# Stick-breaking attention with a fixed TensorE order, paired heads and three units of lookahead

## The chip, the cores and the metric

The program runs on one core of a Trainium2 chip. The metric is the device time of one execution in microseconds, the median of several runs. Its engines, each with an instruction queue of its own, are TensorE (PE; its weight loads are the rows PEld), VectorE (DVE), ScalarE (ACT), GpSimd (POOL) and SyncE (SP), which issues the transfers.

## The reference, cut to what matters

A transformer of two layers, width 1024, sequence 2048. The first layer mixes three kinds of attention; the change touches one of them, stick-breaking, in 6 of its 16 heads. For a block of 128 queries, z are the scaled scores; the weight of a key is sigmoid(z) times the product of sigmoid(-z) over all later keys that are still before the query:

```python
strict = key_idx[None, :] < q_idx[:, None]
log_1mb = jnp.where(strict, jax.nn.log_sigmoid(-z), 0.0)
rc = jnp.flip(jnp.cumsum(jnp.flip(log_1mb, axis=-1), axis=-1), axis=-1)
after = rc - log_1mb
w = jnp.where(strict, jnp.exp(jax.nn.log_sigmoid(z) + after), 0.0)
return jnp.einsum('bhqk,bkhd->bqhd', w.astype(v.dtype), v)
```

## The kernel before, in words

Two layers are written as a row of stages. The stick-breaking stage, `stick_breaking`, follows the projections of layer 0 and is followed by `differential`. It loops over 3 pairs of heads (p), 4 chunks of 512 queries (t, from 3 down to 0), 4 blocks of 128 queries in a chunk (qi) and the chunks of up to 512 keys (c) at or below the diagonal, the last one first. One pass of the innermost loop, for both heads of the pair, is called a **unit** here: 120 of them, 84 of 512 keys, and 12 each of 384, 256 and 128 keys. A **block** is 128 queries by 128 keys of one head; the stage has 816.

For each head a unit does the following (names as in the rows below):

- the scores `psz` = queries (`qs`) times keys (`kv`), two matmuls into one PSUM bank, and on the 48 diagonal units a third that adds the mask (L572, L575);
- on ScalarE, `wb` = sigmoid(z) into SBUF (L577) and sigmoid(-z) in place in PSUM (L578);
- on VectorE, a scan from the last key to the first that keeps the running product in `row` (L581); its second operand is a broadcast zero in SBUF;
- `wb` times `row` (L585), four times on GpSimd and once on VectorE in turn (`"PPPPV"`);
- the transposes of the 128x128 blocks into one PSUM bank `pstp` on TensorE (`tblocks`, L474) and their copy into `wT`, on ScalarE (L121) and VectorE (L123) in turn (`"AV"`);
- `pspv` += values times `wT` (L591), two matmul records per block.

At the end of a chunk VectorE multiplies `pspv` by the loaded gate `sl` (L595) and the result is stored. PSUM's eight banks are z 4, tp 3, pv 1; SBUF has 5 buffers each of `row`, `wb` and `wT`.

A scheduler orders each engine's instructions, TensorE's among them, from the program and its own estimate of times. So rows of other work can stand between those of this stage: `filler` prepares `differential`, and its casts of output weights (`wo`, L871 on ScalarE) are drawn up to the start of the stage. A `PinnedCore` wrapper, already in use in `differential`, keeps the named engines in the order of the program; instructions sent through it carry the helper's line (L57 in the changed kernel).

Of the kernel before, what the change touches and what calls it, by code (L numbers as in the profile page):

```python
# [7 lines left out]
F32 = mybir.dt.float32  # L8
# [3 lines left out]
AF = mybir.ActivationFunctionType  # L12
ALU = mybir.AluOpType
# [4 lines left out]
P = 128  # L18
NB = S // P
TC = 512  # L20
NT = S // TC
# [11 lines left out]
FT = 1  # L33
# [3 lines left out]
GROUPS = ((), (), (0, 1), (2, 3), (4,), (), (), (), (5, 6))  # L37
EVAC_C = "A"
FILL = 0.95
PRODUCTS = ((), (0, 1), (), (2, 3))  # L40
SHUF_D = [4, 5, 6, 7, 0, 1, 2, 3] + list(range(8, 32))
SHUF_S = [8, 9, 10, 11, 12, 13, 14, 15, 0, 1, 2, 3, 4, 5, 6, 7] + list(range(16, 32))
# [22 lines left out]
class Net:  # L65
# [47 lines left out]
    def turn(self, key, pattern):  # L113

        k = self.turns.get(key, 0)
        self.turns[key] = k + 1
        return pattern[k % len(pattern)]
# [164 lines left out]
    def layer1_proj(self):  # L282
        nc, dr = self.nc, self.dr
# [3 lines left out]
        ws = [w0, w1]  # L287
# [29 lines left out]
        for k, dst in enumerate((0, 1, self.sbq[1], self.sbk[1], self.sbq[2], self.sbk[2])):  # L317
            w = nxt
            for t in range(NT):
                ps = self.proj_t(w, t)  # L320
                if k < 2:
                    q = self.t("c2")
                    nc.scalar.mul(q, ps, 0.125)
                    for hh in range(2):
                        qs = self.t("c2", F32R)
# [14 lines left out]
        ws = [nxt, None]  # L340
# [10 lines left out]
        for p in range(3):  # L351
            for base, dst in ((9, self.dfq), (12, self.dfk)):
                w = nxt
                for t in range(NT):
# [3 lines left out]
                    hi = self.t("c2", F32R)  # L358
                    lo = self.t("c2", F32R)
# [5 lines left out]
                           [(f, t) for f in range(6) for t in range(NT)] + [(f, t) for t in range(NT) for f in (6, 7)])  # L365
        for k, _ in enumerate(gates):
            if k == 24 + GATES_A:
                self.sb_first = self.load_sb(0)

    def rope_all(self):  # L370

# [154 lines left out]

    def load_sb(self, p):

        qs = self.load_qstack(self.sbq[p], NT - 1)
        ks = [self.t("kv", F32R) for _ in range(2)]  # L530
        n = S if p else TC
        for lo in range(S - n, -1, -n):
            for hh in range(2):
                for part in range(2):
                    self.dma(ks[hh][64 * part:64 * part + 64, lo:lo + n], self.sbk[p][part, 64 * hh:64 * hh + 64, lo:lo + n])
        vp = self.t("kv", F32, [P, NB, P])
        self.dma(vp, self.v1[:, :, p * P:(p + 1) * P].rearrange("b k f -> k b f"))
        return ks, vp, qs

    def stick_breaking(self):  # L540
        nc = self.nc
        for p in range(3):
            ks, vp, qs = self.load_sb(p) if p else self.sb_first
            for t in range(NT - 1, -1, -1):
                if p == 2 and t == FT:
                    self.fill = self.filler()
                    for f in next(self.fill):
                        f()
                    self.dk, self.dq = {}, {}
                    self.load_dq(0, 0, 0)  # L550
                    for c in range(NT - 1):
                        self.load_dk(0, c)
                if t < NT - 1:
                    qs = self.load_qstack(self.sbq[p], t)
                sl = self.load_silu(self.silu[p], t)
                pv = self.psum("pv")
                for qi in range(3, -1, -1):
                    qb = 4 * t + qi
                    qcol = slice(qi * P, (qi + 1) * P)
                    n = (qb + 1) * P  # L560
                    pr = [self.t("row") for _ in range(2)]
                    for hh in range(2):
                        nc.gpsimd.memset(pr[hh][:, n - 1:n], 1.0)
                    for c in range(qb // 4, -1, -1):
                        lo, hi = c * 512, min(n, c * 512 + 512)
                        m = hi - lo
                        ws = []
                        for hh in range(2):
                            z = self.psum("z")
                            diag = hi == n  # L570
                            for k in range(2):
                                nc.tensor.matmul(z[:, :m], qs[:, hh, k, qcol], ks[hh][:, lo:hi], start=(k == 0),  # L572
                                                 stop=(k == 1 and not diag))
                            if diag:
                                nc.tensor.matmul(z[:, m - P:m], self.identb, self.mask[:, 2 * P + 1:3 * P + 1], start=False, stop=True)  # L575
                            w = self.t("wb")
                            nc.scalar.activation(w[:, :m], z[:, :m], AF.Sigmoid, scale=0.125)  # L577
                            nc.scalar.activation(z[:, :m], z[:, :m], AF.Sigmoid, scale=-0.125)  # L578
                            s0 = 1 if lo == 0 else 0
                            prr = pr[hh]  # L580
                            nc.vector.tensor_tensor_scan(  # L581
                                prr[:, lo + s0 - 1:hi - 1][:, ::-1], z[:, s0:m][:, ::-1], self.zero.to_broadcast([P, m - s0]),
                                prr[:, hi - 1:hi], ALU.mult, ALU.add)
                            eng = nc.gpsimd if self.turn("mul", "PPPPV") == "P" else nc.vector
                            eng.tensor_mul(w[:, :m], w[:, :m], prr[:, lo:hi])  # L585
                            ws.append(w)
                        wT = [self.tblocks([w[:, j * P:(j + 1) * P] for j in range(m // P)]) for w in ws]
                        for j in range(m // P):
                            blk = c * 4 + j
                            for hh in range(2):  # L590
                                nc.tensor.matmul(pv[64 * hh:64 * hh + 64, qcol], vp[:, blk, 64 * hh:64 * hh + 64],  # L591
                                                 wT[hh][:, j * P:(j + 1) * P],
                                                 start=(hi == n and j == 0), stop=(c == 0 and j == m // P - 1))
                mt = self.t("c2")
                nc.vector.tensor_mul(mt, pv, sl)  # L595
                self.dma(self.m1[p, :, t * TC:(t + 1) * TC], mt, nc.scalar if p == 2 and t == 0 else None)

    def differential(self):

# [763 lines left out]
    def run(self):  # L1363
        nc, dr, i = self.nc, self.dr, self.i
        with self.phase({"kv": 6, "qs": 2}, {}):
            with self.phase({"big": 8, "w": 13, "c2": 9, "mv": 2}, {"mm": 3, "z": 2, "tp": 2, "pv": 1}):
                self.layer1_proj()
            right = ExitStack()
            right.enter_context(self.phase({"rx": 3, "mp": 5, "wo": 5, "kc": 3, "qa": 2}, {}, "right"))
            with self.phase({"row": 5, "wb": 5, "wT": 5, "c2": 2, "sl": 2}, {"z": 4, "tp": 3, "pv": 1}, "right"):  # L1370
                self.stick_breaking()
        self.rp = dr.tile([NB, P, D], F32, name="rp")
        self.silu2 = [dr.tile([P, S], F32, name=f"silu2_{f}") for f in range(8)]
        self.m2 = dr.tile([8, P, S], F32, name="m2")
        with self.phase({"c2": 3, "sl": 2}, {}):
            with self.phase({"qd": 2, "wT": 7, "vc": 4, "row": 9, "kd": 3},
                            {"mm": 1, "z": 3, "tp": 2, "pv": 2}):
                tail = self.differential()
            right.close()
            with self.phase({"big": 16}, {}):  # L1380
                with self.phase({"w": 4, "raw": 1}, {"mm": 5, "tp": 3}):
                    with self.phase({"ex": 1, "m": 2, "mp": 4, "rx": 5, "gb": 2}, {}):
                        self.join(tail)
                    with self.phase({"w": 6, "cs": 2, "c2": 7}, {}):
                        self.layer2_kv()
                        for _ in self.gates(i["wo"][11:19], self.silu2, order=[(f, t) for f in range(2, 7) for t in range(NT)] + [(7, 3), (7, 0)]):
# [80 lines left out]
```

## Time and profile before

| | us |
|---|---|
| median of 3 runs (lowest to highest) | 2593.26 (2591.59 to 2594.64) |
| profiled execution: its time | 2590.89 |
| profiled execution: its span | 2589.1 |
| stick-breaking stage, from 720 to 1117 of the span | 397 |

The profiled execution stands for 0.09% less than the median. The stage is one part of the whole program, so shares over the whole span say little about it; the rows below are cut to its window. Busy times of TensorE come from pipelined matmuls whose ends are modelled, so that a PE near 100% busy is not a PE at its peak. "Idle before" of a group is the time for which its engine had nothing to do just ahead of it, with what ended that wait.

### The profile page before, as it was taken

The numbers are of one execution on the slowest core, as the hardware profiler recorded it, in microseconds if no ns is written. First come the engines' busy times: TensorE is split into PE (matmuls) and PEld (weight loads), VectorE is DVE, ScalarE is ACT, GpSimd is POOL, SyncE is SP. The second block draws the span as 40 slices with busy tenths as digits, with TensorE's granted clock in tenths as the row PEclk, the third lists the DMA queues.
The fourth block names the chain that finished last, engine by engine and source line by source line (L and its number), as shares of the span: only waits on it lengthen the run. The fifth ranks groups of instructions, "written<-read, shape, count | busy, mean of one in ns | idle before, by whom it ended". The sixth has DMA issues, their size and how long they took to land. (4 is left out here: it accounts for less than half of the span.)

```text
span 2589.1 us, 42439 instructions
## 1 busy us (share of the span) xinstructions
PE 2450.0 (95%) x15564; PEld 1952.1 (75%) x15564; DVE 1626.6 (63%) x3744; ACT 1261.8 (49%) x2653; POOL 897.5 (35%) x752
## 2 busy tenths in 40 slices
PE   8999999999979999989888889899999999999998
PEld 7778998888857777757666667778788777777887
DVE  4833223531159999979899899795311776677455
ACT  4442222221147777747777677543211777776200
POOL 0401003750036655620110121364621655534333
PEclk9999999999989999989999999999999999999999
DMA  7643222331571422263454332463323555523541
GB/s 287 208 158 129 74 84 90 126 126 48 140 177 42 107 50 50 58 161 99 107 123 123 99 98 63 147 207 128 82 90 116 146 161 155 149 93 106 194 146 65
DMA packets 199247, 311.59 MB, mean 120 GB/s; under 512 B 17920, under 2 KB 97280, under 8 KB 198528
## 3 DMA queue, kind: packets, MB, share of 16 engines
q1 hardware_dynamic: 198464, 307.83, 40.2%
q8 instruction: 123, 2.02, 0.3%
q10 hardware_dynamic: 576, 1.05, 0.1%
q14 instruction: 84, 0.69, 0.1%
HBM read 204.74 MB, written 104.07 MB: 119 GB/s over the span
## 5 line engine op out<-in xcount | busy, mean ns | idle before, releaser
L55 PE MATMUL psmm<-big,w 128*128 128x512 f32 x1680 | 413.8, 394 | 0.0
L55 PEld LDWEIGHTS psmm<-big,w 128*128 128x128 f32 x1680 | 305.8, 189 | 57.6
L581 DVE TENSOR_TENSOR_SCAN row<-psz,row,zero 128x512 f32<-128x512 f32 (+5 forms) x240 | 258.6, 1108 | 34.1 <-ACT psz L578 33.8
L252 PE MATMUL psmm<-big,w 128*128 128x512 f32 x1200 | 275.2, 389 | 0.0
L585 POOL TENSOR_TENSOR wb<-wb,row 128x512 f32<-128x512 f32 (+3 forms) x192 | 219.3, 1152 | 133.0 <-DVE row L581 123.1
L252 PEld LDWEIGHTS psmm<-big,w 128*128 128x128 f32 x1200 | 225.0, 188 | 47.0 <-issue 0.2
L55 PE MATMUL psmm<-big,mp 128*128 128x512 f32 x1056 | 245.0, 392 | 1.4 <-POOL big L962 1.4
L55 ACT ACTIVATE row<-row,mn 128x2048 f32<-128x2048 f32 (+7 forms) x192 | 229.8, 1202 | 11.8 <-DVE mn L728 7.3
L55 PEld LDWEIGHTS psmm<-big,mp 128*128 128x128 f32 x1056 | 198.4, 189 | 43.0 <-POOL big L962 1.8
L722 DVE TENSOR_SCALAR_CACHE_REDUCE row<-psz 128x512 f32<-128x512 f32 (+1 forms) x324 | 200.5, 639 | 25.1 <-PE psz L55 24.5
L1181 DVE TENSOR_TENSOR c<-psmm,c 128x512 f32<-128x512 f32 x62 | 42.7, 691 | 240.3 <-ACT c L1180 240.2
L55 ACT COPY wT<-pstp 128x512 f32<-128x512 f32 (+3 forms) x240 | 121.0, 522 | 116.7 <-PE pstp L55 114.0
L591 PE MATMUL pspv<-wT,kv 128*64 128x128 f32 x1632 | 158.0, 287 | 17.2 <-ACT wT L121 17.2
L892 POOL TENSOR_TENSOR mp<-mp,mp 128x640 fp32r<-128x640 f32 x32 | 52.2, 1632 | 347.4 <-ACT mp L55 297.3
L577 ACT ACTIVATE wb<-psz 128x512 f32<-128x512 f32 (+3 forms) x240 | 129.8, 541 | 53.5 <-PE pstp L474 38.4
L591 PEld LDWEIGHTS pspv<-wT,kv 128*64 128x64 f32 x1632 | 106.7, 139 | 62.3 <-issue 20.7
L572 PE MATMUL psz<-kv,qs 128*128 128x512 f32 (+3 forms) x480 | 150.0, 406 | 2.1 <-DVE row L581 2.0
L55 PE MATMUL psmm<-wo,mp 128*128 128x512 f32 x480 | 148.0, 421 | 3.2 <-ACT mp L55 2.5
L764 DVE SCALAR_TENSOR_TENSOR row<-row,tiny,row 128x128 f32<-128x128 f32 (+7 forms) x144 | 149.9, 1090 | 0.4
L1180 ACT ACTIVATE c<-psmm 128x512 f32<-128x512 f32 x62 | 36.7, 596 | 211.7 <-PE psmm L252 203.8
L207 POOL TENSOR_TENSOR w<-w,w 128x1024 fp32r<-128x1024 f32 x20 | 48.6, 2432 | 257.5 <-ACT w L206 154.5
L55 PE MATMUL pstp<-ident,row 128*128 128x128 f32 x816 | 130.1, 280 | 6.6 <-ACT wT L55 5.6
(220 smaller groups left out, 5073.6 us busy)
## 6 DMA issues: line engine op xcount, KB each, us to landing
silu<-c SPq DMA_DIRECT2D x54, 256.0 KB, 2.3
sl<-silu SPq DMA_DIRECT2D x54, 256.0 KB, 3.2
qs<-sbq SPq DMA_DIRECT2D x48, 256.0 KB, 5.3
cs<-rope SPq DMA_DIRECT2D x24, 512.0 KB, 4.4
kc<-k SPq DMA_DIRECT2D x36, 320.0 KB, 5.0
w<-in_we_dram SPq DMA_DIRECT2D x20, 512.0 KB, 3.7
raw<-in_wo_dram SPq DMA_DIRECT2D x20, 512.0 KB, 3.9
rx<-in_x_dram SPq DMA_DIRECT2D x32, 256.0 KB, 2.8
```

What stands on the lines that cost most here:

```text
L55: return self.tc.keep_in_program_order(f(*a, **k))
L207: eng.tensor_sub(lo[:, sl], raw[:, sl], hi[:, sl].bitcast(F32))
L252: self.nc.tensor.matmul(ps, w[a][:, c, :], self.xpart(t, c, b), start=(c == k == 0), stop=(c == 7 and k == 2))
L572: nc.tensor.matmul(z[:, :m], qs[:, hh, k, qcol], ks[hh][:, lo:hi], start=(k == 0), stop=(k == 1 and not diag))
L577: nc.scalar.activation(w[:, :m], z[:, :m], AF.Sigmoid, scale=0.125)
L581: nc.vector.tensor_tensor_scan(prr[:, lo + s0 - 1:hi - 1][:, ::-1], z[:, s0:m][:, ::-1], self.zero.to_broadcast([P, m - s0]), prr[:, hi - ...
L585: eng.tensor_mul(w[:, :m], w[:, :m], prr[:, lo:hi])
L591: nc.tensor.matmul(pv[64 * hh:64 * hh + 64, qcol], vp[:, blk, 64 * hh:64 * hh + 64], wT[hh][:, j * P:(j + 1) * P], start=(hi == n and j == ...
L722: nc.vector.tensor_scalar(e[:, col + lo:col + lo + n0], z[:, :n0], -scale, before, ALU.mult, ALU.min, accum_out=acc)
L764: self.nc.vector.scalar_tensor_tensor(x[:, lo:hi], y[:, lo:hi], cf[hh][:, w:w + 1], x[:, lo:hi], ALU.mult, ALU.add)
L892: self.nc.gpsimd.tensor_sub(ml, m, mh.bitcast(F32))
L1181: nc.vector.tensor_mul(sg, ps, sg)
```

## The change

The stage is written as three functions over a flat list of units: `scores` (matmuls, sigmoids, scan, product), `turn` (transposes and their copies) and `values`. `scores` runs three units ahead of `turn`; `values` follows for two units at a time. TensorE is pinned to this order. The two heads' scores stand in one tile of two banks, so that one ACTIVATE of up to 128x1024 does both heads; the second sigmoid goes into an SBUF tile `s` and not back into PSUM; the zeros of the scan are a PSUM tile; all products are on GpSimd; two copies of three are on ScalarE (`"AAV"`). The queries of the next chunk are loaded at the start of a chunk, and the keys and values of the next pair at the start of t = 2.

```python
-                            w = self.t("wb")
-                            nc.scalar.activation(w[:, :m], z[:, :m], AF.Sigmoid, scale=0.125)
-                            nc.scalar.activation(z[:, :m], z[:, :m], AF.Sigmoid, scale=-0.125)
...
-                                prr[:, lo + s0 - 1:hi - 1][:, ::-1], z[:, s0:m][:, ::-1], self.zero.to_broadcast([P, m - s0]),
...
-                            eng = nc.gpsimd if self.turn("mul", "PPPPV") == "P" else nc.vector
-                            eng.tensor_mul(w[:, :m], w[:, :m], prr[:, lo:hi])
...
+        self.nc = PinnedCore(nc, self.tc, ("tensor",))
...
+        def begin(p, t):
+            sls[p, t] = self.load_silu(self.silu[p], t)
+            k = chunks.index((p, t)) + 1
+            if k < len(chunks):
+                qs[chunks[k]] = self.load_qstack(self.sbq[chunks[k][0]], chunks[k][1])
+            if t == NT - 2 and p < 2:
+                kv[p + 1] = self.load_sb(p + 1)
...
+            z = self.psum("z", [P, 2, 512])
+            for hh in range(2):
+                for k in range(2):
+                    self.nc.tensor.matmul(z[:, hh, :m], qs[p, t][:, hh, k, qi * P:(qi + 1) * P], kv[p][0][hh][:, lo:hi], start=(k == 0),
+                                          stop=(k == 1 and not diag))
...
+            w = ws[u] = self.t("wb", F32, [P, 2, 512])
+            nc.scalar.activation(w[:, :, :m], z[:, :, :m], AF.Sigmoid, scale=0.125)
+            rest = self.t("s", F32, [P, 2, 512])
+            nc.scalar.activation(rest[:, :, :m], z[:, :, :m], AF.Sigmoid, scale=-0.125)
+            for hh in range(2):
+                prr = prs[p, t, qi][hh]
+                nc.vector.tensor_tensor_scan(
+                    prr[:, lo + s0 - 1:hi - 1][:, ::-1], rest[:, hh, s0:m][:, ::-1], zero.to_broadcast([P, m - s0]),
+                    prr[:, hi - 1:hi], ALU.mult, ALU.add)
+                nc.gpsimd.tensor_mul(w[:, hh, :m], w[:, hh, :m], prr[:, lo:hi])
...
+            wTs[u] = [self.tblocks([w[:, hh, j:j + P] for j in range(0, hi - lo, P)], "AAV") for hh in range(2)]
...
+        for u in units[:SB_AHEAD]:
+            scores(u)
+        for k, u in enumerate(units):
+            if k + SB_AHEAD < len(units):
+                scores(units[k + SB_AHEAD])
+            turn(u)
+            while k - done >= SB_GROUP or k == len(units) - 1 and done <= k:
+                for v in units[done:done + SB_GROUP]:
+                    values(v)
+                done += SB_GROUP
...
-            with self.phase({"row": 5, "wb": 5, "wT": 5, "c2": 2, "sl": 2}, {"z": 4, "tp": 3, "pv": 1}, "right"):
+            with self.phase({"row": 4, "wb": 4, "s": 3, "wT": 7, "c2": 2, "sl": 2}, {"z": 2, "tp": 2, "pv": 1, "zero": 1}, "right"):
```

TensorE's queue before, in the first chunk of the first pair (waits on semaphores in brackets, named by the engine that signals):

```order
L572 MATMUL psz_6580<-kv_5725,qs_6520 128x512 [waits DVE_49]
L572 MATMUL psz_6580<-kv_5725,qs_6520 128x512
L474 MATMUL pstp_6495<-ident,wb_6482 128x128 [waits PE_49,Pool_49]
L474 MATMUL pstp_6495<-ident,wb_6482 128x128 x3
L591 MATMUL pspv_5908<-wT_6462,kv_5742 64x128 [waits Activation_49]
L572 MATMUL psz_6610<-kv_5724,qs_6520 128x512 [waits DVE_49]
L572 MATMUL psz_6610<-kv_5724,qs_6520 128x512
L591 MATMUL pspv_5908<-wT_6469,kv_5742 64x128 [waits DVE_49]
L591 MATMUL pspv_5908<-wT_6462,kv_5742 64x128
```

Scores of one head, transposes and values of another unit follow one another in an order that the scheduler chose; a score tile waits for the scan (VectorE) that read its bank. In the changed kernel the queue at that place reads:

```order
L57 MATMUL pstp_6080<-ident,wb_5968 128x128 [waits Activation_49,Pool_49]
L57 MATMUL pstp_6080<-ident,wb_5968 128x128 x3
L57 MATMUL pstp_6087<-ident,wb_5968 128x128 [waits DVE_49,Pool_49]
L57 MATMUL pstp_6087<-ident,wb_5968 128x128 x3
L57 MATMUL psz_6094<-kv_5724,qs_5719 128x512 x2
L57 MATMUL psz_6094<-kv_5725,qs_5719 128x512 x2
L57 MATMUL pstp_6107<-ident,wb_6001 128x128 [waits Activation_49,Pool_49]
L57 MATMUL pstp_6107<-ident,wb_6001 128x128 x2
L57 MATMUL pstp_6113<-ident,wb_6001 128x128 [waits Activation_49,Pool_49]
L57 MATMUL pstp_6113<-ident,wb_6001 128x128 x2
L57 MATMUL pspv_6050<-wT_6041,kv_5742 64x128
L57 MATMUL pspv_6050<-wT_6048,kv_5742 64x128
```

Here both heads' transposes stand together, each waiting for the copy that freed its `pstp` tile (two tiles in all) and for the product; the scores of a later unit stand between the transposes of two units, and the values of two units behind the second.

ScalarE's queue before, at that place:

```order
L577 ACTIVATE wb_6156<-psz_6153 128x512 [waits Pool_49]
L578 ACTIVATE psz_6153<-psz_6153 128x512 [waits DVE_49]
L577 ACTIVATE wb_6186<-psz_6183 128x512 [waits DVE_49,PE_49]
L578 ACTIVATE psz_6183<-psz_6183 128x512 [waits DVE_49]
L121 COPY wT_6128<-pstp_6123 128x512 [waits PE_49]
L577 ACTIVATE wb_6194<-psz_6191 128x512 [waits Pool_49]
L578 ACTIVATE psz_6191<-psz_6191 128x512 [waits DVE_49]
```

And in the changed kernel (L591 and L593 are its two sigmoids, L123 its copy, L909 the cast of an output weight):

```order
L123 COPY wT_6041<-pstp_6036 128x512 [waits PE_49]
L909 CAST wo_9784<-rx_9776 128x512 [waits DMAHW3_49]
L591 ACTIVATE wb_6072<-psz_6067 128x1024 [waits PE_49,Pool_49]
L593 ACTIVATE s_6074<-psz_6067 128x1024 [waits DVE_49,Activation_49]
L123 COPY wT_6085<-pstp_6080 128x512 [waits PE_49]
L123 COPY wT_6092<-pstp_6087 128x512 [waits PE_49,Activation_49]
L591 ACTIVATE wb_6099<-psz_6094 128x1024 [waits PE_49,Pool_49]
```

One pair of wide sigmoids takes the place of two pairs; a unit's copies stand behind the sigmoids of the unit three further on, and ahead of those of the fourth. The casts stay at the start of the stage.

## Rows read from the trace of the kernel before

**Rows 1.** Windows: us; busy (x) of PE, PEld, DVE, ACT, POOL; PEclk; DMA share; GB/s

```profile
720.00:760.00 40.00, 21.05 (x123) 14.59 (x122) 18.09 (x20) 16.50 (x33) 15.33 (x19) 0.79 1.00 228
760.00:1117.00 357.00, 356.65 (x2907) 257.86 (x2905) 334.59 (x402) 261.25 (x574) 217.36 (x275) 0.99 0.25 59
720.00:1117.00 397.00, 377.71 (x3028) 272.45 (x3026) 352.69 (x421) 277.75 (x607) 232.68 (x293) 0.97 0.32 76
```

**Rows 2.** Lines, 720 to 1117: count | busy us, mean ns | idle before, what ended it

```profile
L581 DVE TENSOR_TENSOR_SCAN row<-psz,row,zero 128x512 f32<-128x512 f32 (+5 forms) x240 | 258.6, 1108 | 34.1 <-ACT psz L578 33.8
L585 POOL TENSOR_TENSOR wb<-wb,row 128x512 f32<-128x512 f32 (+3 forms) x192 | 219.3, 1152 | 133.0 <-DVE row L581 123.1 <-PE pspv L591 4.4 <-PE pstp L474 4.0
...
L123 DVE COPY wT<-pstp 128x512 f32<-128x512 f32 (+3 forms) x120 | 70.5, 591 | 7.5 <-PE pstp L474 7.0
...
L585 DVE TENSOR_TENSOR wb<-wb,row 128x512 f32<-128x512 f32 (+3 forms) x48 | 34.3, 714 | 1.0
```

**Rows 3.** Waits, 760 to 1117: who waited for what, us in total, times, longest

```profile
POOL wb L585 <- DVE row L581: 119.9, 116, 3.7
ACT wT L121 <- PE pstp L474: 39.9, 62, 2.1
...
DVE row L581 <- ACT psz L578: 22.1, 25, 6.8
PEld pstp L474 <- issue: 20.8, 120, 0.3
```

**Rows 4.** Lines by form, ScalarE alone, 720 to 1117

```profile
L578 ACT ACTIVATE psz<-psz 128x512 f32<-128x512 f32 x168 | 101.7, 606 | 0.0
L577 ACT ACTIVATE wb<-psz 128x512 f32<-128x512 f32 x168 | 101.7, 605 | 45.9 <-PE pstp L474 36.7 <-PE psz L572 7.3 <-PE psz L575 0.9
L121 ACT COPY wT<-pstp 128x512 f32<-128x512 f32 x84 | 49.6, 591 | 33.0 <-PE pstp L474 32.0
...
L577 ACT ACTIVATE wb<-psz 128x128 f32<-128x128 f32 x24 | 6.7, 281 | 5.8 <-POOL wb L585 2.6 <-PE psz L575 1.5 <-PE pstp L474 1.3
```

**Rows 5.** Timeline of ScalarE, first 40 us: start, duration, instruction, [idle before]

```profile
739.43 1.66 ACT L871 CAST wo<-rx 128x512 fp32r<-128x512 f32 x3 [12.96 <-DMA m<-c]
...
757.67 0.62 ACT L871 CAST wo<-rx 128x512 fp32r<-128x512 f32 x1 [6.68 <-DMA rx<-in_woute_dram]
```

**Rows 6.** Timeline of all engines, 849 to 863

```profile
849.83 0.71 PE L572 MATMUL psz<-kv,qs 128*128 128x512 f32 x2
...
850.63 0.60 ACT L577 ACTIVATE wb<-psz 128x512 f32<-128x512 f32 x1 [0.78 <-PE psz L572]
...
851.13 0.59 ACT L578 ACTIVATE psz<-psz 128x512 f32<-128x512 f32 x1
...
851.49 0.66 PE L474 MATMUL pstp<-ident,wb 128*128 128x128 f32 x4
...
852.43 1.21 PE L572 MATMUL psz<-kv,qs 128*128 128x512 f32 x4
...
853.65 0.65 PE L591 MATMUL pspv<-wT,kv 128*64 128x128 f32 x6
...
855.88 0.33 PE L474 MATMUL pstp<-ident,wb 128*128 128x128 f32 x1
...
857.03 1.09 PE L591 MATMUL pspv<-wT,kv 128*64 128x128 f32 x14
```

**Rows 7.** Instructions of L585: duration ns min/median/max, first and last start, forms

```profile
L585 POOL TENSOR_TENSOR wb<-wb,row x192: 454/1273/1367, 724.2 to 1114.0; 128x512 f32<-128x512 f32 x144, 128x256 f32<-128x256 f32 x18, 128x384 f32<-128x384 f32 x15, 128x128 f32<-128x128 f32 x15
...
L585 DVE TENSOR_TENSOR wb<-wb,row x48: 280/692/1153, 729.3 to 1114.8; 128x512 f32<-128x512 f32 x24, 128x384 f32<-128x384 f32 x9, 128x128 f32<-128x128 f32 x9, 128x256 f32<-128x256 f32 x6
```

**Rows 8.** Lines by form, 760 to 1117: full-width scan, product, transposes

```profile
L585 POOL TENSOR_TENSOR wb<-wb,row 128x512 f32<-128x512 f32 x137 | 173.6, 1276 | 110.8 <-DVE row L581 102.9 <-PE pspv L591 4.4 <-PE pstp L474 3.0
...
L474 PE MATMUL pstp<-ident,wb 128*128 128x128 f32 x783 | 129.2, 284 | 0.0
...
L581 DVE TENSOR_TENSOR_SCAN row<-psz,row,zero 128x512 f32<-128x512 f32 x83 | 104.2, 1272 | 16.0 <-ACT psz L578 15.9
```

More of the change, by code (lines that the diff above doesn't have):

```diff
@@ L39 @@
 FILL = 0.95
+SB_AHEAD = 3
+SB_GROUP = 2
 PRODUCTS = ((), (0, 1), (), (2, 3))
@@ L367, in layer1_proj @@
             if k == 24 + GATES_A:
-                self.sb_first = self.load_sb(0)
+                qs = self.load_qstack(self.sbq[0], NT - 1)
+                self.sb_first = (*self.load_sb(0), qs)
     def rope_all(self):
@@ L527, in load_sb @@
     def load_sb(self, p):
-        qs = self.load_qstack(self.sbq[p], NT - 1)
         ks = [self.t("kv", F32R) for _ in range(2)]
@@ L537, in load_sb @@
         self.dma(vp, self.v1[:, :, p * P:(p + 1) * P].rearrange("b k f -> k b f"))
-        return ks, vp, qs
+        return ks, vp
     def stick_breaking(self):
         nc = self.nc
[L542 to L575, printed above, removed]
-                            w = self.t("wb")
-                            nc.scalar.activation(w[:, :m], z[:, :m], AF.Sigmoid, scale=0.125)
-                            nc.scalar.activation(z[:, :m], z[:, :m], AF.Sigmoid, scale=-0.125)
-                            s0 = 1 if lo == 0 else 0
-                            prr = pr[hh]
-                            nc.vector.tensor_tensor_scan(
-                                prr[:, lo + s0 - 1:hi - 1][:, ::-1], z[:, s0:m][:, ::-1], self.zero.to_broadcast([P, m - s0]),
-                                prr[:, hi - 1:hi], ALU.mult, ALU.add)
-                            eng = nc.gpsimd if self.turn("mul", "PPPPV") == "P" else nc.vector
-                            eng.tensor_mul(w[:, :m], w[:, :m], prr[:, lo:hi])
[L586 to L593, printed above, removed]
@@ new lines, in stick_breaking @@
+        self.nc = PinnedCore(nc, self.tc, ("tensor",))
+        chunks = [(p, t) for p in range(3) for t in range(NT - 1, -1, -1)]
+        units = [(p, t, qi, c) for p, t in chunks for qi in range(3, -1, -1) for c in range(t, -1, -1)]
+        kv, qs, sls, prs, ws, wTs, pvs = {0: self.sb_first[:2]}, {(0, NT - 1): self.sb_first[2]}, {}, {}, {}, {}, {}
+        def begin(p, t):
[5 more added lines that the diff above has]
+                kv[p + 1] = self.load_sb(p + 1)
+            if p == 2 and t == FT:
+                self.fill = self.filler()
+                for f in next(self.fill):
+                    f()
+                self.dk, self.dq = {}, {}
+                self.load_dq(0, 0, 0)
+                for c in range(NT - 1):
+                    self.load_dk(0, c)
@@ new lines, in bounds, with scores @@
+        def bounds(u):
+            p, t, qi, c = u
+            n = (4 * t + qi + 1) * P
+            return n, c * 512, min(n, c * 512 + 512)
+        def scores(u):
+            p, t, qi, c = u
+            n, lo, hi = bounds(u)
+            m, diag, s0 = hi - lo, hi == n, int(lo == 0)
+            if qi == 3 and c == t:
+                begin(p, t)
+            if c == t:
+                prs[p, t, qi] = [self.t("row", F32, [P, 2048]) for _ in range(2)]
+                for hh in range(2):
+                    nc.gpsimd.memset(prs[p, t, qi][hh][:, n - 1:n], 1.0)
+            z = self.psum("z", [P, 2, 512])
[3 more added lines that the diff above has]
+                                          stop=(k == 1 and not diag))
+                if diag:
+                    self.nc.tensor.matmul(z[:, hh, m - P:m], self.identb, self.mask[:, 2 * P + 1:3 * P + 1], start=False, stop=True)
+            w = ws[u] = self.t("wb", F32, [P, 2, 512])
+            nc.scalar.activation(w[:, :, :m], z[:, :, :m], AF.Sigmoid, scale=0.125)
+            rest = self.t("s", F32, [P, 2, 512])
+            nc.scalar.activation(rest[:, :, :m], z[:, :, :m], AF.Sigmoid, scale=-0.125)
+            for hh in range(2):
+                prr = prs[p, t, qi][hh]
[3 more added lines that the diff above has]
+                nc.gpsimd.tensor_mul(w[:, hh, :m], w[:, hh, :m], prr[:, lo:hi])
@@ new lines, in turn, with values @@
+        def turn(u):
+            n, lo, hi = bounds(u)
+            w = ws.pop(u)
+            wTs[u] = [self.tblocks([w[:, hh, j:j + P] for j in range(0, hi - lo, P)], "AAV") for hh in range(2)]
+        def values(u):
+            p, t, qi, c = u
+            n, lo, hi = bounds(u)
+            if qi == 3 and c == t:
+                pvs[p, t] = self.psum("pv")
+            pv, wT, nj = pvs[p, t], wTs.pop(u), (hi - lo) // P
+            for j in range(nj):
+                for hh in range(2):
+                    self.nc.tensor.matmul(pv[64 * hh:64 * hh + 64, qi * P:(qi + 1) * P], kv[p][1][:, 4 * c + j, 64 * hh:64 * hh + 64],
+                                          wT[hh][:, j * P:(j + 1) * P], start=(hi == n and j == 0), stop=(c == 0 and j == nj - 1))
+            if qi == 0 and c == 0:
@@ L594, in stick_breaking @@
                 mt = self.t("c2")
-                nc.vector.tensor_mul(mt, pv, sl)
+                nc.vector.tensor_mul(mt, pvs.pop((p, t)), sls.pop((p, t)))
                 self.dma(self.m1[p, :, t * TC:(t + 1) * TC], mt, nc.scalar if p == 2 and t == 0 else None)
+        done = 0
+        zero = self.psum("zero")[:, :1]
+        nc.vector.memset(zero, 0.0)
+        for u in units[:SB_AHEAD]:
[8 more added lines that the diff above has]
+                done += SB_GROUP
@@ L598, in differential @@
+        self.nc = nc
     def differential(self):
```

## The prediction

> **What bounds the kernel now.** I read the windows first, since shares over the whole program mix stages. The stage takes 397 us, of which VectorE is busy 352.69; in the stretch from 760 to 1117 it is busy 334.59 of 357, or 94% [rows 1]. TensorE reads as busy all the time there, but its matmuls are pipelined, so that says little. GpSimd is busy 217 us, ScalarE 261.
>
> The lines and the waits tell the same engine from the other side. GpSimd's 133 us of idle time before its products end almost all with a scan of VectorE [rows 2]; in the stretch it waits for `row` 116 times, 119.9 us in all [rows 3]. ScalarE waits for transposes (39.9 us ahead of its copies), which wait for products. VectorE itself waits 22.1 us for a sigmoid [rows 3]. So VectorE sets the pace: 258.6 us of scans, 70.5 of copies, 34.3 of products [rows 2]. The reader should see one engine that hardly waits and others that wait for it.
>
> The first 40 us are another matter: VectorE is busy 18 us of them [rows 1], and ScalarE stands twice behind a cast of output weights whose data has not landed, for 12.96 and 6.68 us [rows 5]. These casts stand at the stage's start in the changed order too, behind the same loads, so I give this stretch no gain and no loss, within 3 us.
>
> **The change part by part.** *VectorE* loses its 48 products (34.3 us) and 40 of its 120 copies (one in three instead of one in two: 70.5/3 = 23.5 us) [rows 2]. That is 57.8 us, of which 97% lie in the stretch: 334.6 - 56 = 279 us. It would no longer be full.
>
> *GpSimd* gets those 48 products. Its own cost 1152 ns in the mean [rows 2], so 48 x 1.15 = 55 us, and 217 + 54 = 271 us in the stretch. That lies beside the rest as long as the stretch stays longer than that.
>
> *ScalarE.* No 1024-wide sigmoid is in the trace. From 128 to 512 columns one goes from 281 to 605 ns [rows 4], 0.844 ns a column, so 1024 columns give 605 + 512 x 0.844 = 1037 ns. Consecutive ones start 0.50 apart [rows 6], 0.1 less than one lasts, so about 0.93 for the pair of heads. The price has two sides: two of today's take 2 x 0.50 = 1.00, and a fixed share (281 - 128 x 0.844 = 173 ns) saved whole and not overlapped at all would make it 1.00 - 0.17 = 0.83. I take 0.93, as the line through two widths is nearest. ScalarE also gets 40 more copies at 0.53 to 0.59 us [rows 4]; with 1.87 for the sigmoids and 4/3 x 0.5 for copies it has some 2.5 us of work for a full unit.
>
> *The second sigmoid into SBUF.* The first writes SBUF, the second PSUM, and they take 605 and 606 ns [rows 4]. I take nothing. The Trainium skill says otherwise: "ScalarE: Activation LUTs", section "Step-by-step: what each stage is for", calls PSUM the faster destination, and "Perfetto Trace Analysis", section "Optimizing Scalar/DVE Operations", gives ScalarE about 93 ns of overhead on SBUF and about 51 on PSUM. By those figures 60 such sigmoids in the loop below would add an estimated 60 x 0.042 = 2.5 us, and the sum would be 2562 and not 2560; the measured pair shows no such difference.
>
> *The fixed order makes a loop,* and I take its length for the new pace, because VectorE and GpSimd now have slack. TensorE's order for two units is scores(j+3), transposes(j), scores(j+4), transposes(j+1), values of two units, scores(j+5). Transposes(j+1) need a `pstp` tile, of which there are only two, both used by transposes(j); they come free with the copies of j. These copies stand in ScalarE's queue behind both sigmoids of j+3, and those wait for scores(j+3), which stand behind the values before them. So once in two units all of this lies end to end, for full units, in us:
>
> - four score matmuls 1.21, and 0.09 until the sigmoid starts (849.83 + 0.71 to 850.63) [rows 6]
> - the two sigmoids 0.93 + 0.94
> - a copy 0.59 [rows 4], and 0.10 until the transposes start
> - transposes of two heads: four take 0.66 and one 0.33 [rows 6], so 0.11 each, 8 x 0.11 = 0.88
> - values of two units, 32 records: fourteen take 1.09, six 0.65 [rows 6], so 0.055 each, 1.75
>
> The sum is 6.49 us. In one of three cycles the copy that is waited for is VectorE's and lies beside the sigmoids, which makes about 0.44 less: 6.34 in the mean, for 16 blocks. The stage has 60 such cycles, but its units are 6.8 blocks of 8 wide in the mean. Some 0.9 us of a cycle does not shrink with the width (three ScalarE instructions at 0.17, the handoffs 0.2, and 0.2 for the ends of matmul groups, an estimate); the rest does: 0.9 + 0.85 x 5.44 = 5.52, and 0.11 for masks makes 5.63. 60 x 5.63 = 338 us for 816 blocks, 0.414 each. The stretch has 783 transposes [rows 8] in 357 us, 0.456 each now; at 0.414 it is 324 us, **33 us less**. The engines fit: VectorE 279 and GpSimd 271 of 324.
>
> This takes the wide sigmoid's two prices to 60 x 2 x 0.07 = 8 us more and 60 x 2 x 0.10 = 12 us less.
>
> *What I cost at nothing.* Scan and product of a unit take place in the three units (some 8 us) before its transposes: scan 1.27 twice and product 1.28 behind the second [rows 8], about 4 us; if that cover went, the transposes would wait and with them everything behind them on TensorE. Zeros in PSUM: the scan already reads one operand there at 1.27, so nothing, above or below, but for the third rival. The queries' load for the next chunk has a chunk's time, at least 4 units, to land. The memsets of `row` stand in GpSimd's queue behind products of earlier units; with 3 units of lead that is covered too.
>
> Sum against the profiled execution: 2590.89 - 33 = 2558; the median is 2.4 above that execution, so **2560**.
>
> **The rivals.**
>
> *The loop has slack, and VectorE stays the pace.* If ScalarE's copies are not what the transposes wait for, VectorE at today's share gives 279/0.94 = 298 us, 59 less: 2534. TensorE's own work is a floor under it: two more score matmuls take 1.21 - 0.71 = 0.50 [rows 6], so two units take 2 x (1.00 + 0.88 + 0.87) = 5.5, times 0.85, plus 0.11 and 0.2 as above, 4.99 for 13.6 blocks or 0.367 each: 287 us, 70 less: 2523. For it speaks that waits in a chain of four engines seldom all lie end to end; against it that two `pstp` tiles leave no room.
>
> *The gain turns into waits of TensorE.* Pinned, TensorE can't take other work when an operand is late. Today its weight loads show 0.17 us of "issue" at an exposed start (20.8 us in 120 times) [rows 3]. Four such a cycle, one at each change of kind, would be 0.68 x 60 = 41 us: 0.464 a block, 363 us, 6 more than now, 2599; with two, 2579. Against it: some of them are already in the times that I added.
>
> *The other side: VectorE's scan and GpSimd's product lock each other out.* Two operands of VectorE in SBUF seem to meet GpSimd: VectorE's own products, both inputs in SBUF, spread from 280 to 1153 ns around a median of 692, and GpSimd's from 454 to 1367 [rows 7]. The scan now takes its factors from SBUF, where before they were in PSUM. If a scan and a product can't overlap, a full unit costs two of each in a row, 2 x 1.27 + 2 x 1.28 = 5.1 us, 0.638 a block, 499 us, or 142 more: about 2735. It decides from 0.456 a block, that is once a fifth of them ((0.456 - 0.414)/(0.638 - 0.414)) no longer lie beside each other. Against it: the scan's zero was in SBUF and is now in PSUM, so it has one SBUF operand as before, and with that the full scan took 1272 ns and the full product 1276 [rows 8] beside each other. The Trainium skill's "Perfetto Trace Analysis", section "Optimizing Scalar/DVE Operations", warns that moving work between the two might not help as they share a read port; "SBUF — State Buffer", section "Who interferes with whom", limits that to VectorE instructions with two SBUF inputs (or in a two-port mode), and the rows so far agree with the narrower rule.
>
> **How the numbers follow.** The forecast, 2543 to 2575, has 0.50: its bounds are the wide sigmoid's +8 and -12, 3 of the start and some 5 for the estimate of what doesn't shrink. The first rival has 0.26 (2515 to 2543), the second 0.18 (2575 to 2605), the third 0.06. Within 0.2%, or 5.2 us, of the median is about what a measurement can't tell from no change. Of the second rival 0.07 is faster than that, 0.06 within it, 0.05 slower; the rest follows: faster 0.83, same 0.06, slower 0.11. For the range I go from 2526, which keeps 0.21 of the first rival, to 2590, which keeps 0.10 of the second: 0.81 together.
>
> **What would show it right or wrong.** The stage near 364 us, with VectorE below 88% busy and without products; ScalarE's 1024-wide sigmoids at 1.04; scan and product still at 1.27 and 1.28 (over 1.4 means the third rival); transposes that wait for ScalarE's copies, not for products, and little idle on GpSimd. If VectorE is 94% busy and its waits short, the first rival is right. If weight loads show "issue" before most groups and the stage is as long as now, the second is. A first stretch that changes by more than 3 us, by other positions of the casts, would be a mistake ahead of all this.

## The result and the profile after

The changed kernel takes 2578.44 us in the median of four runs (2573.72 to 2583.06), against 2593.95 for the kernel before in the same series: ratio 0.9941, interval 0.9921 to 0.9961, 15.5 us less. The sign and the range were right; the forecast gain of 33 us was more than twice too large. The profiled execution, which the next paragraphs take apart, took 2579.35 us (span 2577.6), 11.5 less than that of before.

Windows of the changed kernel; the columns are those of [rows 1]:

```profile
720.00:760.00 40.00, 20.18 (x100) 15.04 (x99) 16.50 (x17) 16.10 (x22) 18.18 (x19) 0.70 0.99 237
760.00:1098.00 338.00, 307.46 (x2935) 245.97 (x2934) 283.39 (x317) 253.11 (x385) 255.43 (x323) 1.00 0.26 61
```

The stage ends at 1098.4 instead of 1117.2, 18.8 us earlier. VectorE is down from 94 to 84% (283.39 of 338), as forecast. TensorE, which was busy 356.65 of 357 us, is busy 307.46 of 338 for slightly more instructions. It is busy 49 us less and has some 30 us of waits, which leaves 19. Waits of TensorE's matmuls, first before, then after, from 760 to 1098 in both (who waited for what, us, times, longest):

```profile
PE psz L572 <- DVE row L581: 0.3, 1, 0.3
```

```profile
PE pstp L57 <- ACT wT L123: 20.8, 33, 1.2
PE pstp L57 <- DVE wT L125: 4.9, 9, 1.5
PE pstp L57 <- POOL row L582: 2.8, 5, 0.9
PE pstp L57 <- POOL wb L599: 1.6, 3, 0.8
```

Before, TensorE had no wait worth the name; now its transposes wait for copies. Their weight loads also wait for products:

```profile
PEld pstp L57 <- POOL wb L599: 24.5, 30, 1.9
```

But the copy comes last: 25.7 of the 30.1 us of matmuls' waits above end with one. Lines by form of the changed kernel from 760 to 1098, which answer to [rows 4] and [rows 8]:

```profile
L591 ACT ACTIVATE wb<-psz 128x1024 f32<-128x1024 f32 x79 | 82.1, 1039 | 55.3 <-PE psz L57 50.3 <-POOL wb L599 2.7 <-POOL row L582 2.0
L593 ACT ACTIVATE s<-psz 128x1024 f32<-128x1024 f32 x79 | 81.7, 1035 | 0.0
...
L599 POOL TENSOR_TENSOR wb<-wb,row 128x512 f32<-128x512 f32 x160 | 201.7, 1284 | 77.2 <-DVE row L596 76.8
...
L596 DVE TENSOR_TENSOR_SCAN row<-s,row,pszero 128x512 f32<-128x512 f32 x82 | 100.3, 1267 | 32.3 <-ACT s L593 31.8 <-POOL row L582 0.5
```

The 1024-wide sigmoids take 1039 and 1035 ns (forecast 1037); scans and products are where they were. One cycle of two units, from 918.35 to 925.15, on the timeline of TensorE and ScalarE (start, duration, instruction, idle before):

```profile
918.35 1.20 PE L57 MATMUL psz<-kv,qs 128*128 128x512 f32 x4
919.38 1.04 PE L57 MATMUL pstp<-ident,wb 128*128 128x128 f32 x8
919.64 1.03 ACT L591 ACTIVATE wb<-psz 128x1024 f32<-128x1024 f32 x1 [2.00 <-PE psz L57]
920.18 1.17 PE L57 MATMUL psz<-kv,qs 128*128 128x512 f32 x4
920.57 1.02 ACT L593 ACTIVATE s<-psz 128x1024 f32<-128x1024 f32 x1
921.47 1.08 ACT L123 COPY wT<-pstp 128x512 f32<-128x512 f32 x2
922.20 1.12 PE L57 MATMUL pstp<-ident,wb 128*128 128x128 f32 x8 [0.86 <-ACT wT L123]
...
923.25 1.97 PE L57 MATMUL pspv<-wT,kv 128*64 128x128 f32 x32
...
925.15 0.50 PE L57 MATMUL psz<-kv,qs 128*128 128x256 f32 x2
```

This is the loop that the prediction described. Scores to sigmoid 1.29, sigmoids 0.93 and 0.90, copy to transposes 0.73, transposes to values 1.05, values to the next scores 1.90: 6.80 us, where the prediction had 1.30, 0.93, 0.94, 0.69, 0.88 and 1.75, or 6.49.

### The profile page after: what moved, and what is told of

It reads as the page before. It is cut to its first block, busy times and chain, and to the rows that moved or that the text cites. A ratio compares the mean times of both kernels' runs of the same rounds, so it can differ in the third digit from the quotient of the medians.

```text
span 2577.6 us, 42239 instructions
## 1 busy us (share of the span) xinstructions
PE 2406.5 (93%) x15564; PEld 1946.7 (76%) x15564; DVE 1574.5 (61%) x3657; ACT 1253.4 (49%) x2453; POOL 943.8 (37%) x800
## 3 DMA queue, kind: packets, MB, share of 16 engines
q10 hardware_dynamic: 576, 1.05, 0.1%
## 5 line engine op out<-in xcount | busy, mean ns | idle before, releaser
L599 POOL TENSOR_TENSOR wb<-wb,row 128x512 f32<-128x512 f32 (+3 forms) x240 | 263.0, 1119 | 83.9 <-DVE row L596 83.0
L596 DVE TENSOR_TENSOR_SCAN row<-s,row,pszero 128x512 f32<-128x512 f32 (+5 forms) x240 | 252.8, 1103 | 58.6 <-ACT s L593 57.9
L57 PE MATMUL pstp<-ident,wb 128*128 128x128 f32 x816 | 118.7, 279 | 36.1 <-ACT wT L123 25.9
L57 PE MATMUL psz<-kv,qs 128*128 128x512 f32 (+3 forms) x480 | 134.9, 399 | 14.3 <-ACT s L593 14.3
L591 ACT ACTIVATE wb<-psz 128x1024 f32<-128x1024 f32 (+3 forms) x120 | 109.2, 910 | 79.7 <-PE psz L57 72.5
L57 PEld LDWEIGHTS pstp<-ident,wb 128*128 128x128 f32 x816 | 91.0, 142 | 63.2 <-POOL wb L599 26.0
```

Of the source, the lines that this page charges most:

```text
L57: return self.tc.keep_in_program_order(f(*a, **k))
L591: nc.scalar.activation(w[:, :, :m], z[:, :, :m], AF.Sigmoid, scale=0.125)
L596: nc.vector.tensor_tensor_scan(prr[:, lo + s0 - 1:hi - 1][:, ::-1], rest[:, hh, s0:m][:, ::-1], zero.to_broadcast([P, m - s0]), prr[:, hi ...
L599: nc.gpsimd.tensor_mul(w[:, hh, :m], w[:, hh, :m], prr[:, lo:hi])
```

## Experiments

Runs e1 to e4 shared one chip, where the kernel before took 2590.0 us; the others shared one where it took 2591 to 2592. So ratios to the kernel before are compared; the changed kernel's is 0.9941.

**e1: values behind the next scores.**

```diff
-            turn(u)
-            while k - done >= SB_GROUP or k == len(units) - 1 and done <= k:
+            while k - 1 - done >= SB_GROUP:
                 for v in units[done:done + SB_GROUP]:
                     values(v)
                 done += SB_GROUP
+            turn(u)
+        for v in units[done:]:
+            values(v)
```

> The changed kernel with one edit: the values of two units are issued behind the next scores, not ahead of them. Theory A (transposes wait for the copies of the unit before, these stand behind two sigmoids, and those wait for scores that stand behind the values): the 1.75 to 2.0 us of values leave that loop, a cycle of two units falls from the measured 5.9 us towards TensorE's own 5.0 to 5.5, so the stretch from 760 on loses 20 to 45 us and the time is 2535 to 2560. Theory B (products come late, three units of lead are too short): the order of values changes nothing that the transposes wait for, within 5 us of the changed kernel's 2578.

2566.41 us, ratio 0.9908 (0.9893 to 0.9923), an interval that just touches the changed kernel's. The trace is clearer: from the scores of the ninth unit to those of the 117th, 54 cycles, it takes 305.8 us, 5.66 a cycle; the changed kernel takes 317.2, or 5.87. So the values were in the loop, against Theory B, but the gain is well under Theory A's 20 to 45: another wait stood close behind. The largest group of waits of TensorE's matmuls in e1, from 765 to 1080, is for VectorE's copies in place of ScalarE's:

```profile
PE pstp L57 <- DVE wT L125: 20.9, 16, 2.3
```

**e6: as e1, all copies on ScalarE.**

```diff
-            wTs[u] = [self.tblocks([w[:, hh, j:j + P] for j in range(0, hi - lo, P)], "AAV") for hh in range(2)]
+            wTs[u] = [self.tblocks([w[:, hh, j:j + P] for j in range(0, hi - lo, P)], "A") for hh in range(2)]
```

> The kernel with the values behind the next scores (run e1_values_late), and in addition all copies of transposes on ScalarE. Theory A continued: with the values out of the loop, what TensorE waits for is VectorE's copies, which stand behind scans (20.9 us in 16 waits in e1_values_late); then the time falls from 2566 by 6 to 18, to 2548 to 2560, with VectorE near 235 us busy. Rival: ScalarE, now with every copy besides its sigmoids (about 297 us of work at start-to-start times), becomes the bound, and the time is 2564 or more.

2541.13 us, ratio 0.9801 (0.9786 to 0.9816): 25 us less than e1 by the medians and some 28 by the ratios, more than expected, with 5.33 us a cycle. VectorE's copies queue behind pairs of scans, 2.45 us long; on ScalarE they don't. From 760 to 1067, where e6's stage ends:

```profile
760.00:1067.00 307.00, 298.09 (x2933) 246.56 (x2932) 244.79 (x240) 284.50 (x463) 252.95 (x322) 1.00 0.29 67
```

TensorE is busy 97% again, with ScalarE at 93%.

**e11: the same edit alone,** TensorE's order as in the changed kernel.

> The changed kernel with one edit: all copies of transposes on ScalarE, the order of TensorE unchanged (values ahead of the next scores). Theory A: in every cycle the copy that is waited for now stands behind both sigmoids, so cycles of full units with the copy on VectorE (6.31 us in the trace) become like those with it on ScalarE (6.81), and the time rises by 5 to 15, to 2583 to 2593. Rival: VectorE's copies behind scans are the wait that matters in this order too, then it falls as it did with the values moved, to 2553 to 2568.

2585.32 us, ratio 0.9974 (0.9960 to 0.9988): slower than the changed kernel, as Theory A has it. The two intervals just touch, and the traces agree with the medians: every cycle now has the copy behind both sigmoids, and the mean over the 53 cycles from the ninth unit on is 6.05 us, against 5.90 in the changed kernel. The same edit that gains some 28 us once the values are out of the loop costs some 9 (0.0033 of 2592) while they are in it.

**e12: TensorE not pinned.**

```diff
-        self.nc = PinnedCore(nc, self.tc, ("tensor",))
```

> The changed kernel without the pin on TensorE: the scheduler orders it again. If the fixed order brings nothing by itself and the relief of VectorE made the gain, the time stays within 6 of 2578. If the fixed order is what keeps copies and transposes apart, it rises above 2590; if the fixed order costs by its loop, it falls below 2570.

2602.19 us, ratio 1.0038 (1.0028 to 1.0048). **e13: the kernel before, all products on GpSimd.**

```diff
-                            eng = nc.gpsimd if self.turn("mul", "PPPPV") == "P" else nc.vector
+                            eng = nc.gpsimd if self.turn("mul", "P") == "P" else nc.vector
```

> The kernel before with one part of the change alone: all products on GpSimd. If VectorE, 94% busy, sets the pace there, it loses 34 us of work and the time falls by 15 to 34, to 2557 to 2576. If what VectorE is waited for is its place in the chain of a unit and not its load, a product on GpSimd (1.28 instead of 0.70 us) lengthens that chain and the time is 2588 or more.

2599.40 us, ratio 1.0030 (1.0018 to 1.0043). These two bear on what bounded the kernel before. Their windows, e12 first:

```profile
760.00:1123.00 363.00, 361.52 (x2933) 264.22 (x2931) 285.29 (x317) 261.46 (x387) 255.46 (x322) 1.00 0.24 57
```

```profile
760.00:1117.00 357.00, 355.67 (x2868) 258.51 (x2868) 307.86 (x354) 262.89 (x573) 256.82 (x319) 0.99 0.24 58
```

In e13 VectorE falls from 334.59 to 307.86 us in the same 357, and nothing is gained; in e12 it falls to 285 of 363, with all other parts of the change in place, and the stage is longer than before. In both TensorE is busy over 99% and its matmuls hardly wait: 0.7 us in e12 and 1.2 in e13, from 760 to 1098. So VectorE's load was not the bound; TensorE in the scheduler's order was. The other outcome expected of e13, a longer chain of a unit through GpSimd, would give the same time; against it stand these short waits, and e12, where the pin on TensorE alone makes some 25 us (0.9941 against 1.0038). The fixed order alone, on the kernel before, was not tried.

**e4: every fifth product on VectorE again** in the changed kernel (`"PPPPV"` in place of GpSimd alone).

> The changed kernel with every fifth product on VectorE again. If VectorE's relief is what made the gain, its busy time in the stage rises by about 34 us from 300 and the time by 10 to 15, to about 2590. If the loop over ScalarE's copies sets the pace (Theory A), VectorE has room for it (283 + 31 of 338 us) and the time stays within 5 of 2578.

2585.85 us, ratio 0.9984 (0.9972 to 0.9997), some 11 us above the changed kernel. This is the outcome expected of VectorE's relief, and Theory A missed it. In the profiled execution, the fastest of e4's, the stage ends only some 2.5 us later, but the 54 cycles counted under e1 take 323.2 us against 317.2. Transposes wait longer for VectorE's copies, which stand in the loop (e4 from 760 to 1098; the changed kernel has 4.9 us in 9 waits):

```profile
PE pstp L57 <- DVE wT L125: 13.7, 18, 2.1
```

So in the fixed order it does pay to keep VectorE free. Where the rest of the 11 us arises is not shown.

**e3: zeros in SBUF.**

```diff
-        zero = self.psum("zero")[:, :1]
-        nc.vector.memset(zero, 0.0)
+        zero = self.zero
```

> The changed kernel with the scan's zeros back in SBUF (the bank is left unused), so that the scan has two operands in SBUF. If a scan with two SBUF operands and a product of GpSimd lock each other out, scans and products of 512 columns rise well over 1.4 us or wait for each other, and the time goes above 2620. If a broadcast of one zero does not count as such an operand, both stay at 1.27 and 1.28 and the time at 2578 within 5.

2684.10 us, ratio 1.0364 (1.0347 to 1.0381). Lines by form of e3 from 765 to 1080:

```profile
L599 POOL TENSOR_TENSOR wb<-wb,row 128x512 f32<-128x512 f32 x116 | 231.0, 2018 | 27.1 <-DVE row L596 27.1
L596 DVE TENSOR_TENSOR_SCAN row<-s,row,zero 128x512 f32<-128x512 f32 x62 | 105.4, 1743 | 5.8 <-ACT s L593 5.8
```

The scan rises from 1267 to 1743 ns and the product from 1284 to 2018, though the second operand is one broadcast zero per partition. The prediction's third rival is a real mechanism, worth some 110 us here (1.0364 - 0.9941 of 2592); the changed kernel avoids it by the bank that it gives to the zeros. The Trainium skill's "SBUF — State Buffer", section "Who interferes with whom", says that a VectorE instruction with two SBUF inputs contends with a GpSimd instruction that reads SBUF, and one with a single SBUF input does not; these rows agree with both halves.

**e8: second sigmoid back in PSUM, zeros in SBUF,** two transpose tiles; **e9:** the same with the free bank as a third tile.

```diff
-            rest = self.t("s", F32, [P, 2, 512])
+            rest = z
...
-        zero = self.psum("zero")[:, :1]
-        nc.vector.memset(zero, 0.0)
+        zero = self.zero
```

> The changed kernel with the second sigmoid back in place in PSUM and the scan's zeros back in SBUF; transposes keep two tiles and one bank stays unused. Scans then have one operand in SBUF and should take 1.27 again, unlike in e3_zero_sbuf. But a score tile is held until both heads' scans have read it: if two score tiles are then too few, scores wait for scans and the time is 2590 to 2620; if the scans are early enough, it stays within 6 of 2578.

> As e8_sig_psum, with the free bank as a third tile for transposes. Theory A says that two tiles for transposes close the loop over the copies: the third lets one head's transposes go ahead of the copies of the unit before, and the time is 5 to 20 under e8_sig_psum. If the tiles are not what transposes wait for, the two are within 4 of each other.

e8 takes 2593.17 us, ratio 1.0006 (0.9995 to 1.0017); e9 2590.13, ratio 0.9990 (0.9978 to 1.0003). The second sigmoid takes as long as in SBUF (1024 ns, and 1028 for the first). But scores now wait for scans, in e8 from 765 to 1080:

```profile
PEld psz L57 <- DVE row L596: 27.6, 46, 1.7
PE psz L57 <- DVE row L596: 18.4, 32, 1.4
```

So the copy in SBUF is worth some 17 us by the ratios, by freeing the score tile early. Full scans and products are at 1271 and 1279 ns in e8, with the zeros in SBUF and the factors in PSUM, so it is the scan's second operand in SBUF that costs in e3, and not the place of the zeros. The third transpose tile brings no gain that these runs can tell (the intervals overlap), and not the 5 to 20 us that Theory A gave it; with score tiles as the tighter wait, e9 says little on Theory A.

**e2: ScalarE pinned as well,** with the two sigmoids issued through the pinned wrapper.

```diff
-        self.nc = PinnedCore(nc, self.tc, ("tensor",))
+        self.nc = PinnedCore(nc, self.tc, ("tensor", "scalar"))
```

> The changed kernel with ScalarE pinned to the program's order as well: the casts of output weights then stand at the third pair's t = 1 and not at the start of the stage. If the 20 us in which ScalarE stands behind these casts in the first 40 us are time lost by the whole stage, the time falls by 10 to 20 us, to 2558 to 2568. If the first 40 us are held by the loads of keys and values themselves (all transfer engines are busy there), it stays within 4 us of 2578.

2564.00 us, ratio 0.9901 (0.9883 to 0.9918). The ninth unit's scores start at 743.6 instead of 765.5. The stretch from 720 to 760, which answers to the first window above:

```profile
720.00:760.00 40.00, 34.83 (x297) 27.64 (x296) 33.29 (x37) 31.33 (x44) 29.63 (x35) 0.96 0.87 204
```

TensorE starts three times as many matmuls in it (297 for 100). Some 10 of these 22 us are lost later: the chunk in which the casts now stand takes 33.2 us from its first scores to those of the next chunk, against 22.5, with ScalarE waiting for the same loads there:

```profile
1044.35 0.62 ACT L57 CAST wo<-rx 128x512 fp32r<-128x512 f32 x1 [5.52 <-DMA rx<-in_woute_dram]
```

**e7: e1, e2 and the casts one unit apart.** The program keeps the four first loads of `filler` at t = 1 of the third pair and issues the rest one step a unit:

```diff
-                for f in next(self.fill):
-                    f()
+                first.extend(next(self.fill))
+                for f in first[:4]:
+                    f()
+                del first[:4]
...
+            if first:
+                since.append(k)
+                if len(since) > 3:
+                    first.pop(0)()
```

> Both edits that gained: values behind the next scores, ScalarE pinned; and the casts of output weights issued one unit apart at the third pair's t = 1 instead of in one burst. If the loop's 12 us and the start's 22 us (first score of the ninth unit at 743.6 instead of 765.5) are separate costs, they add and the burst's 10 us stay away: 2541 to 2553. If the start's gain is only work moved into a loop that is bound elsewhere, it ends at 2556 to 2564, no better than the better of the two.

2550.42 us, ratio 0.9836 (0.9819 to 0.9852). That is 0.0105 under the changed kernel, where e1 and e2 alone gain 0.0033 and 0.0040: the two costs add, and the chunk with the casts takes 22.5 us again, so that e2's loss there is saved.

**e10: e7 with all copies on ScalarE.**

> All that gained together: values behind the next scores, all copies of transposes on ScalarE, ScalarE pinned, casts of output weights one unit apart at the third pair's t = 1. If the costs are separate, e7_late_pin_spread's 16 us over e1_values_late come on top of e6_late_copies_act's 2541: 2520 to 2530. If ScalarE, which is busy 281 of 300 us there, can't take the casts beside its copies, 2533 to 2541.

2521.59 us, ratio 0.9735 (0.9715 to 0.9756), the fastest of all: 71 us under the kernel before, and some 53 under the changed one by the ratios. Windows of e10:

```profile
720.00:760.00 40.00, 36.37 (x314) 28.62 (x313) 32.85 (x32) 37.49 (x56) 32.02 (x37) 1.00 0.88 204
760.00:1045.00 285.00, 274.92 (x2713) 227.62 (x2713) 226.99 (x223) 264.53 (x432) 240.26 (x304) 1.00 0.32 77
```

## Why the prediction was wrong in size

**What bounded the kernel.** The first step failed: "So VectorE sets the pace". VectorE was busy 94% and others waited for it, but e13 took work off it and gained nothing: TensorE handed out the work at its own pace. This reading did not enter the sum, which starts from the measured 0.456 us a block. The sentence that dismissed the right engine is "TensorE reads as busy all the time there, but its matmuls are pipelined, so that says little". TensorE's busy time per matmul record shows it: 356.65/2907 = 0.123 us before, 361.52/2933 = 0.123 in e12, 355.67/2868 = 0.124 in e13, all in the scheduler's order; 307.46/2935 = 0.105 in the changed kernel and 274.92/2713 = 0.101 in e10. The records' starts, counted in the traces over the same windows, tell where it goes:

```
window            records  changes of kind  same kind next (transposes)  values to transposes
before 760-1117      2905              604                     0.109 us             0.203 us
after  760-1098      2932              287                     0.109 us             0.203 us
e12    760-1123      2932              537                     0.109 us             0.203 us
e13    760-1120      2904              640                     0.109 us             0.203 us
```

(Kinds are scores with masks, transposes and values; the last two columns are medians from one start to the next. The changed kernel goes from values to transposes only twice.)

The fixed order halves the changes from one kind of matmul to another. Not every change costs: scores start 0.028 us after a transpose, in the kernel before and in the changed one. And the count is not all of it. A record of values starts either 0.007 us after the one before, as the second of a pair, or some 0.10 us after it. The 1582 records of values in the window before make 601 such pairs and the 1599 of e12 make 608; the 1598 of the changed kernel make 799, which is all. At 0.096 us for each of the 190 pairs that are missing before, an estimated 18 of the 49 us that TensorE is busy less (356.65 to 307.46) lie there.

That it is the order that gains is shown by e12; how much it gains by fewer changes, and how much by values that start in pairs, is read from these counts, and no run tried either by itself.

The Trainium skill's "Perfetto Trace Analysis", section "Identifying the Most-Contended Engine", sets TensorE's matmul busy share aside and takes the busy share of its weight loads as a measure of headroom. That share was 257.86/357 = 72% before and 227.62/285 = 80% in e10, so headroom there was; but it took another order to use it, and in the order as it was the busy share of 99.9% named the engine that set the pace.

**The parts.** VectorE's and GpSimd's new loads (283 and 255 us, forecast 279 and 271) and the price of the wide sigmoid were near. "*The second sigmoid into SBUF* ... I take nothing" and "Zeros in PSUM ... nothing" held for the instructions' durations. What they buy is more: e8 and e3 price them at some 17 and 110 us. The operand that isn't in SBUF is the third rival, which the prediction named; the score tile that is freed early it did not name. VectorE's relief from products gave nothing in the old order (e13) and some 11 us in the fixed one (e4).

**The loop** was the right mechanism: e1 takes values out of it and gains 9 us by the ratios, 12 by the medians; e11 puts the copy behind the sigmoids in every cycle and loses 9. Its term was mis-sized. "8 x 0.11 = 0.88" and "values of two units ... 1.75" count matmuls by the spacing inside a group; the timeline has 1.05 and 1.90, since the change into values and the one out of them cost gaps of their own, 0.203 us from start to start. That is 0.32 in a cycle of full units. It is the second rival with two exposed starts; the weight loads show both as "issue", at 0.17 us each, nearly once a cycle (760 to 1098):

```profile
PEld psz L57 <- issue: 9.6, 56, 0.2
PEld pspv L57 <- issue: 8.6, 51, 0.2
```

The prediction priced that rival at 2579, and 2578 was measured; so close a match is luck, since only about half of what was missing arose in the loop.

**The sum,** in the profiled pair, 21.5 us short of 33: the stretch from 760 has 792 blocks in 338.4 us, 0.427 each; at 0.414 it would be 328, so 10.4 are the loop. "I give this stretch no gain and no loss" cost 3.8: in the first 40 us the changed kernel does 24 transposes where 33 were done, 9 x 0.427. ScalarE stands behind casts there as before, with a third wait inside the window:

```profile
738.89 1.66 ACT L909 CAST wo<-rx 128x512 fp32r<-128x512 f32 x3 [11.89 <-DMA m<-c]
...
752.63 0.62 ACT L909 CAST wo<-rx 128x512 fp32r<-128x512 f32 x1 [6.04 <-DMA rx<-in_woute_dram]
...
758.14 0.62 ACT L909 CAST wo<-rx 128x512 fp32r<-128x512 f32 x1 [2.09 <-DMA rx<-in_woute_dram]
```

The pin on TensorE is not what loses these 9 transposes: e12, without it, does 24 in this stretch too, and e4, with it, does 38. The granted clock of the stretch is 0.70 against 0.79 before. What the cause is stays open.

The last 7.3 are lost behind the stage, which the prediction didn't count at all: of the 18.8 us gained at its end 11.5 are left at the end of the program. `differential` starts with a load that was issued shortly before the stage's end, first before, then after:

```profile
1122.24 0.59 PE L55 MATMUL psz<-kd,qa 128*128 128x512 f32 x1 [2.58 <-DMA kd<-dfk]
```

```profile
1105.91 0.77 PE L57 MATMUL psz<-kd,qa 128*128 128x512 f32 x1 [5.98 <-DMA kd<-dfk]
```

TensorE waits 3.4 us longer for it, and this matmul starts 16.3 us earlier than before, so that 2.5 of the 7.3 are lost by then. By the starts of the same transposes in both traces, the lead is 14.9 us at 1244 of the span before and 10.8 at 1414; so the rest goes inside `differential`. Why, and why the load takes longer, stays open; no run tried it.

## What to carry to other kernels

An engine that is busy 94% and waited for need not be the bound: take work off it in a run by itself, and look at the engine that never waits, even if its busy time is "only" pipelined. Where TensorE alternates between kinds of matmul, count the changes of kind, look at how closely the records of one kind start, and in a loop written out by hand price each group by the distance from its first start to the next group's, not by its spacing inside. Take the longest group out of the loop first; which engine should do the copies is a question to ask again after that.

## What was not expected of the hardware

A scan with a broadcast zero in SBUF as its second operand, beside its first in SBUF, slowed itself from 1267 to 1743 ns and GpSimd's products from 1284 to 2018. A change from values to transposes on TensorE takes 0.203 us from start to start where one transpose follows another in 0.109; scores follow a transpose in 0.028. Records of values start in pairs 0.007 us apart where the order lets the pairs stand together.
